# Half of the mLSTM values projected between the convolved queries and the convolved keys, with the keys' taps and SiLU moved to the end of the stage

## The chip, the cores and the metric

The kernel runs on one core of a Trainium2 chip, in one launch. The metric is the device time of that core in microseconds (us). Before the change three runs gave 661.01, 662.44 and 662.84 us, median 662.44. The engines are named as in the profile: PE (TensorE, matmuls), PEld (its weight loads), DVE (VectorE), ACT (ScalarE), POOL (GpSimd) and SP (which issues DMAs). L215 is line 215 of the kernel before. In the changed kernel most lines that are spoken of here have a number lower by one (up to L804) or higher by one (L805 to L893).

## The reference, cut to what matters

One layer over 512 tokens of width 1024. Two groups of heads read one projection of the normalised input: an mLSTM group (4 heads, whose queries and keys go through a causal convolution of four taps and a SiLU before use, while the values don't) and an attention group (8 heads, each query block attends to its best keys by an index score). A gated MLP follows, with a convolution of its own.

```
z = h @ w_in[l]
(m_q, m_k, m_v, m_o, m_i, m_f, a_q, a_k, a_v, i_q, i_k, i_w) = split_cols(z, IN_SIZES)
qk = jax.nn.silu(causal_dwconv(jnp.concatenate([m_q, m_k], axis=-1), mlstm_conv_w[l], mlstm_conv_b[l]))
...
hm = mlstm_chunkwise(m_q..., m_k..., m_v..., m_i + i_bias[l], m_f + f_bias[l])
hm = rms_norm(hm, mlstm_norm[l]) ; hm = jax.nn.sigmoid(m_o) * hm
ha = dsa_attention(a_q, a_k, a_v, i_q, i_k, i_w, rel_bias)
x = x + jnp.concatenate([hm, ha], axis=-1) @ w_out[l]
h = rms_norm(x, norm_ffn[l])
u = causal_dwconv(h @ w_up[l], ffn_conv_w[l], ffn_conv_b[l])
x = x + (jax.nn.silu(gate) * val) @ w_down[l]
```

## The kernel before

**Products in three passes.** A float32 weight is split into a high part `whi` (a copy on ACT, L124) and a low part `wlo` (a subtraction, L125, on DVE, or on POOL for the pieces 6 to 24 and a few later ones). Activations are split in the same way (`hh`, `hl`), and each product is hi*hi + lo*hi + hi*lo. Each weight tile of 256 columns gives two pieces. `fm_steps` projects 128 columns for all 512 tokens, features on partitions, in four steps of six matmuls with 512 columns (L215 to L217). `tm_steps` projects 256 columns, tokens on partitions, in eight steps of twelve matmuls with 256 columns (L259 to L261), and needs two pieces at once. Weights are loaded and split in the order in which `add_raw` lists them, ahead of use.

**The order of the work.** `merge` takes a list of main steps (a projection) and lists of side steps. Each side list has a stretch of the main list in fractions, and its steps are laid out evenly in it. A queue `later` gives up one small piece of work per step: the next weight splits and the taps of a convolution. What is written out is the order of each engine, which runs its own list strictly in that order, and waits by semaphores for the others.

**The stage that is changed.** Main steps are four convolution blocks (`to_conv`, 0 and 1 are the mLSTM queries `mq`, 2 and 3 the keys `mk`) of four steps, and then half of the values (`to_mv(0)`, eight steps). A block's last step evacuates PSUM on ACT (L785) and puts three taps on DVE in the queue (L788), each over the whole block. `silus` (both SiLUs, on ACT, and a small memset) stands at 0.7 of the stage. A SiLU and an exponential need different tables on ACT, so that each change of function is an `ACT_TABLE_LOAD`. Side work: the last steps of the top-k of query block 3 (`top3`), the gates (`gate_4` to `gate_7`), the first two `decays`, and all of the attention, `att_steps`.

**The attention** has a software pipeline: step i issues the logits of item i (a query block t and a head h; L701, L702), the biased logits `l` and their row bound `nm` of item i-1 on DVE (L726) with the exponential on ACT (L729), the transposes of item i-3 (L712, copied to `pT` on ACT at L717 or on DVE at L715), and the product with the values of item i-5 (L744). Block 3 takes its bias through `score`, which POOL adds up for each head (L737). At a block's last head DVE takes the reciprocal of the row sums (L748) and writes the output (L751), which frees the only PSUM bank of the products, `bank_av`; the next block's first product waits for it. `second` (L690) subtracts the low part of the queries on DVE.

**PSUM** has two banks `mm`, three `lg`, two `tp` and one `av`; a bank is taken in rotation of its tag. `gate_6` takes two `tp` tiles:

```
pb, pi = bank("tp"), bank("tp")
... nc.tensor.transpose(pi[:4, ...], ig[:, t, :], ident)           # L616
... nc.tensor.matmul(pb[:4, ...], lf[:, t, :], tri_u, ...)          # L618
nc.vector.tensor_tensor_scan(m, m2, pi[:4, :], 0.0, OP.add, OP.max)  # L620
nc.vector.tensor_tensor(m2, pb[:4, :], m, OP.subtract)               # L622
```

**The stage behind it** projects the other half of the values and the output gate. In it come the decays 2 and 3 (a PE broadcast L818, DVE L825 and L829, the exponential L832), the split of `mk` and `mq` into parts (`keys` L859 on ACT, `queries` L868, with subtractions on DVE), and the products `qk` (L881, L882), whose PSUM tile is taken from the three `lg` banks and read by DVE (L884, L887).

Of the kernel before, what the change touches and what calls it, by code (L numbers as in the profile page):

```python
# [28 lines left out]
def merge(main, *sides, later=None):  # L29


    order = [((i + 0.5) / len(main), 0, i, f) for i, f in enumerate(main)]
    for n, (a, b, steps) in enumerate(sides):
        cost = [getattr(f, "cost", 1.0) for f in steps]
        at = np.cumsum(cost) - 0.5 * np.array(cost)
        order += [(a + (b - a) * at[i] / sum(cost), n + 1, i, f) for i, f in enumerate(steps)]
    for _, _, _, f in sorted(order, key=lambda z: z[:3]):
        g = later.popleft() if later else None
        f()
        if g:  # L40
            g()
# [3 lines left out]
def hybrid_layer(ctx: ExitStack, tc: tile.TileContext, a, out):  # L45
# [19 lines left out]
    def mm_bank():  # L65
        mm_tags.append(mm_tags.pop(0))
        return bank(mm_tags[-1])
# [4 lines left out]
    def add_raw(pieces, cuts, place=None):  # L72

        raws.append([pieces, place])
        for view, shape in cuts:
            subs.append([len(raws) - 1, view, shape, None])
# [15 lines left out]
    def merged(main, *sides):  # L92
        merge(main, *sides, later=later)
        while later:
            later.popleft()()
# [31 lines left out]
    def cols(w, ncol, c0, width=256):  # L127
        def pieces(raw):
            dst = raw[:, :8 * width].rearrange("p (k c) -> p k c", k=8)
            src = bass.AP(tensor=w.tensor, offset=w.offset + c0, ap=[[ncol, 128], [128 * ncol, 8], [1, width]])  # L130
            return [(dst, src)]
        return pieces

    def fm_cut(j, width=256):
        return (lambda raw: raw[:, :8 * width].rearrange("p (k c) -> p k c", k=8)[:, :, j * 128:(j + 1) * 128], (8, 128))

    def tm_cut(j):
        return (lambda raw: raw.rearrange("p (k c) -> p k c", k=8)[:, 4 * j:4 * j + 4, :], (4, 256))
# [8 lines left out]
    w_in, DIN, NF = a["w_in"], 3664, DFF // 128  # L147
# [17 lines left out]
    for c0 in (1544, 1800, 2056, 2312):  # L165
        add_raw(cols(w_in, DIN, c0), [fm_cut(0), fm_cut(1)])
    add_raw(cols(w_in, DIN, 2824), [tm_cut(0), tm_cut(1)])
    for c0 in (0, 256):
        add_raw(cols(w_in, DIN, c0), [fm_cut(0), fm_cut(1)])
    for c0 in (512, 768, 1024, 1280):  # L170
        add_raw(cols(w_in, DIN, c0), [tm_cut(0), tm_cut(1)])
    for k0 in (4, 6, 0, 2):
        add_raw(rows(a["w_out"], k0), [row_cut(0), row_cut(1)])
    for c2 in range(NF // 2):
# [31 lines left out]
    def take(n=1):  # L206

        i = sub_i[0]
        sub_i[0] += n
        split_to(i + n)  # L210
        split_soon(i + n + min(look[0], 4 - n))
        return [subs[j][3] for j in range(i, i + n)]

    def mm3(ps_, lh, ll, rh, rl, first, last):
        nc.tensor.matmul(ps_, lh, rh, start=first, stop=False)  # L215
        nc.tensor.matmul(ps_, lh, rl, start=False, stop=False)  # L216
        nc.tensor.matmul(ps_, ll, rh, start=False, stop=last)  # L217

    def fm_steps(act, evac, cols_=128, tok=((0, 512),)):

        st = {}

        def open_():
            (st["w"],) = take()
            st["ps"] = mm_bank()[:cols_, :]

        def part(t0, t1, k0, k1):
            wh, wl = st["w"]
            for k in range(k0, k1):
                mm3(st["ps"][:, t0:t1], wh[:, k, :], wl[:, k, :], act[0][:, k, t0:t1], act[1][:, k, t0:t1],  # L230
                    k == 0, k == 7)

        steps = []
        for t0, t1 in tok:
            n = 2 if t1 - t0 > 256 else 4
            for k in range(0, 8, n):
                steps.append(lambda t0=t0, t1=t1, k=k, n=n: part(t0, t1, k, k + n))
        f0 = steps[0]
        steps[0] = lambda: (open_(), f0())
        last = steps[-1]  # L240
        steps[-1] = lambda: (last(), evac(st["ps"]))
        return steps

    def tm_steps(act, evac):

        st = {}
        steps = []

        def part(t, j):
            if t == 0 and j == 0:  # L250
                st["w"] = take(2)
            if j == 0:
                st["ps"] = mm_bank()[:, :256]
            sl = slice(t * 128, (t + 1) * 128)
            wh, wl = st["w"][j]
            for i in range(4):
                k = 4 * j + i
                ah, al = act[0][:, k, sl], act[1][:, k, sl]
                nc.tensor.matmul(st["ps"], ah, wh[:, i, :], start=(k == 0), stop=False)  # L259
                nc.tensor.matmul(st["ps"], al, wh[:, i, :], start=False, stop=False)  # L260
                nc.tensor.matmul(st["ps"], ah, wl[:, i, :], start=False, stop=(k == 7))  # L261
            if j == 1:
                evac(t, st["ps"])

        for t in range(NB):
            for j in range(2):
                steps.append(lambda t=t, j=j: part(t, j))
        return steps
# [100 lines left out]
    H = (hh, hl)  # L369
# [165 lines left out]
    def top_steps(t):  # L535
        w = (t + 1) * 128
        acc = score[t][:, :w]

        m8 = {}

        def largest():
            m8[0] = small.tile([128, 8], F32, name="m8")
            nc.vector.max(m8[0], acc)

        def strike():
            nc.vector.match_replace(acc, m8[0], acc, TAKEN)

        def fin():
            nc.vector.tensor_scalar(keep[t][:, :w], acc, TAKEN, -BIG, op0=OP.not_equal, op1=OP.mult)
        return [largest, strike] * 16 + [fin]  # L550
# [82 lines left out]
    gates_b = [gate_4, gate_5, gate_6, gate_7]  # L633


    main = []
# [130 lines left out]
    main = []  # L767
# [5 lines left out]
    att_ = att_steps(range(NB))  # L773
    top3 = top_steps(3)
# [7 lines left out]
    def to_conv(c):  # L782
        def evac(pz):
            y = (mq if c < 2 else mk)[:, c % 2, :]
            nc.scalar.activation(y, pz, AF.Identity, bias=cw[:, 4, c:c + 1], scale=cw[:, 3, c:c + 1])  # L785

            def tap(d):
                nc.vector.scalar_tensor_tensor(y[:, d:], pz[:, :S - d], cw[:, 3 - d, c:c + 1], y[:, d:],  # L788
                                               op0=OP.mult, op1=OP.add)
            later.extend(lambda d=d: tap(d) for d in (3, 2, 1))  # L790
        return evac

    def to_mv(c2):
        return lambda t, pz: nc.scalar.activation(mv[:, t, 2 * c2:2 * c2 + 2, :128],
                                                  pz.rearrange("p (h d) -> p h d", h=2), AF.Copy)
# [3 lines left out]
    def to_mo(c2):  # L799
        return lambda t, pz: nc.vector.tensor_copy(past[0][:, t, c2 * 256:(c2 + 1) * 256], pz)  # L800

    def silus():
        nc.gpsimd.memset(mv[:, :, :, 128:130], 1.0)
        nc.scalar.activation(mq, mq, AF.Silu)  # L804
        nc.scalar.activation(mk, mk, AF.Silu)  # L805


# [84 lines left out]
    decays, parts, qks = weight_steps()  # L892
    mm_tags[:] = ["mm"]  # L893
    main = []
    for c in range(4):
        main += fm_steps(H, to_conv(c))
    main += tm_steps(H, to_mv(0))
    merged(main, (0.0, 0.57, top3[6:]), (0.403, 0.74, gates_b), (0.781, 0.957, decays[:2]), (0.7, 0.7, [silus]), (0.007, 1.0, att_[1:]))


    def head_steps(pair):
# [47 lines left out]
    main = tm_steps(H, to_mv(1))  # L949
# [12 lines left out]
    def out_steps(mix, done, first, last, ahead=4):  # L962


        st = {}
        order = [(t, hf, j) for t in range(NB) for hf in range(2) for j in range(4)]
        if first:
            order[:8] = [(0, hf, j) for j in range(4) for hf in range(2)]
        if last:
            order[24:] = [(NB - 1, hf, j) for j in range(4) for hf in range(2)]  # L970

        def part(t, hf, j):
            if t == 0 and hf == 0 and j == 0:
                st["w"] = take(4)
            if j == 0:
                st[hf] = mm_bank()
            sl = slice(t * 128, (t + 1) * 128)
            wh, wl = st["w"][j]
            nc.tensor.matmul(st[hf], mix[:, 0, j, sl], wh[:, hf, :], start=(j == 0), stop=False)  # L979
            nc.tensor.matmul(st[hf], mix[:, 1, j, sl], wh[:, hf, :], start=False, stop=False)  # L980
            nc.tensor.matmul(st[hf], mix[:, 0, j, sl], wl[:, hf, :], start=False, stop=(j == 3))  # L981
            if t == NB - 1 and hf == 1 and j < ahead:
                split_to(nsplit[0] + 1)
            if j == 3:
                xs = x[t][:, hf * 512:(hf + 1) * 512]
                nc.vector.tensor_tensor(xs, st[hf], xs, OP.add)
                done(t, hf)
        return [lambda z=z: part(*z) for z in order]
# [3 lines left out]
    main = out_steps(mixa, lambda t, hf: None, True, True)  # L992
# [110 lines left out]
    main = g1[:2] + g0[2:] + v0[2:] + g1[2:] + fm_steps(F, to_val(1))  # L1103
# [148 lines left out]
```

## Time and profile before

| | before |
|---|---|
| median of three runs | 662.44 us (661.01 to 662.84) |
| the profiled execution | 661.26 us, of which the span from first to last instruction is 659.5 |
| mean granted clock of PE | 0.994 |
| PE busy | 640.4 us, 97% of the span, 3386 matmuls |
| DVE, ACT, POOL busy | 481.3, 317.0, 169.2 us |
| chain that ended last | PE 82%, DVE 9%, ACT 3%, POOL 2% |

The profiled execution is one run of the program with a hardware profiler. "Busy" adds up instructions; the chain is followed back from the last instruction to what released each step. The stage that is changed ends at 204.5 us of the span; its ninth main step, the first that differs, starts at 146.5 us.

### The profile page before, as it was taken

Reading aid. Unit: us, or ns where it says so; the run is one execution under the profiler, and the core shown is the slowest. Engines: PE = TensorE matmul, PEld = TensorE weight load, DVE = VectorE, ACT = ScalarE, POOL = GpSimd, SP = SyncE. Lnnn points to the kernel's source line nnn. Section 1 sums busy time; section 2 is a strip of 40 time slices with the busy share of each in tenths; the row PEclk is TensorE's granted clock in tenths of the full one; section 3 lists DMA queues with packets and bytes.
Section 4 is the critical chain, followed back from the end, with each engine's and each line's share of the span. In section 5 each row is a group of like instructions: output and inputs, shape, how many; then the busy total and the mean of one; then the engine's idle time right before and its main releaser. Section 6 shows DMA issues by size and latency. Waiting matters only on the chain.

```text
span 659.5 us, 9106 instructions
## 1 busy us (share of the span) xinstructions
PE 640.4 (97%) x3386; PEld 546.8 (83%) x3386; DVE 481.3 (73%) x864; ACT 317.0 (48%) x533; POOL 169.2 (26%) x178
## 2 busy tenths in 40 slices
PE   7999999989999999999999999999999999999994
PEld 5977889868889998889988888888888888888884
DVE  5588999979846866667457665667766678998883
ACT  5546355756675614525344244434344336665561
POOL 2232467221462405325021112121112211000011
PEclk9999999989999999999999999999999999999998
DMA  9421443120110311042354657447664665655542
GB/s 301 117 80 64 141 148 106 54 66 1 64 65 1 130 65 64 6 155 66 125 201 160 215 192 254 178 146 252 192 220 168 229 232 179 231 191 195 186 171 90
DMA packets 58027, 93.95 MB, mean 142 GB/s; under 512 B 4643, under 2 KB 41703, under 8 KB 57856
## 3 DMA queue, kind: packets, MB, share of 16 engines
q1 hardware_dynamic: 50464, 65.49, 29.9%
q0 software_dynamic: 6800, 26.32, 11.3%
q10 hardware_dynamic: 720, 1.57, 0.7%
q8 instruction: 27, 0.44, 0.3%
q14 instruction: 16, 0.13, 0.1%
HBM read 79.72 MB, written 13.65 MB: 142 GB/s over the span
## 4 chain that ended last, share of the span: by engine, by line
PE 82%; DVE 9%; ACT 3%; issue 2%; POOL 2%; DMA 1%; POOLq 0%; DVEq 0%; ACTq 0%
PE bank_mm L215 10%; PE bank_mm L216 10%; PE bank_mm L217 10%; PE bank_av L216 5%; PE bank_av L217 5%; PE bank_av L215 5%; DVE score L528 2%; PE bank_mm L396 2%; PE bank_mm L259 2%; PE bank_mm L979 2%; PE bank_mm L981 2%; PE bank_mm L980 2%; PE bank_tp L1138 2%; PE bank_mm L1138 2%; PE bank_mm L1136 2%
## 5 line engine op out<-in xcount | busy, mean ns | idle before, releaser
L124 ACT ACTIVATE whi<-raw 128x1024 fp32r<-128x1024 f32 x120 | 123.2, 1028 | 69.3 <-PE bank_av L1137 12.6
L125 DVE TENSOR_TENSOR wlo<-raw,whi 128x1024 fp32r<-128x1024 f32 x98 | 117.9, 1206 | 51.1 <-ACT whi L124 51.1
L215 PE MATMUL bank_mm<-fh,whi 128*128 128x512 f32 (+1 forms) x248 | 93.2, 376 | 0.0
L217 PE MATMUL bank_mm<-fh,wlo 128*128 128x512 f32 (+1 forms) x248 | 93.1, 376 | 0.0
L216 PE MATMUL bank_mm<-fl,whi 128*128 128x512 f32 (+1 forms) x248 | 93.1, 375 | 0.0
L125 POOL TENSOR_TENSOR wlo<-raw,whi 128x1024 fp32r<-128x1024 f32 x22 | 54.2, 2468 | 72.0 <-ACT whi L124 56.7
L1051 POOL TENSOR_TENSOR y<-yc 128x512 f32<-128x512 f32 x22 | 30.7, 1397 | 142.0 <-DVE yc L1035 142.0
L215 PEld LDWEIGHTS bank_mm<-fh,whi 128*128 128x128 f32 x248 | 46.7, 188 | 8.5
L217 PEld LDWEIGHTS bank_mm<-fh,wlo 128*128 128x128 f32 x248 | 46.7, 188 | 8.4
L216 PEld LDWEIGHTS bank_mm<-fl,whi 128*128 128x128 f32 x248 | 46.7, 188 | 8.4
L215 PE MATMUL bank_av<-fh,whi 128*128 128x512 f32 (+1 forms) x128 | 48.2, 376 | 0.0
L217 PE MATMUL bank_av<-fh,wlo 128*128 128x512 f32 (+1 forms) x128 | 48.1, 376 | 0.0
L216 PE MATMUL bank_av<-fl,whi 128*128 128x512 f32 (+1 forms) x128 | 48.1, 376 | 0.0
L215 PE MATMUL bank_mm<-hh,whi 128*128 128x512 f32 (+1 forms) x112 | 44.0, 393 | 0.0
L216 PE MATMUL bank_mm<-hl,whi 128*128 128x512 f32 (+1 forms) x112 | 42.3, 378 | 0.0
L217 PE MATMUL bank_mm<-hh,wlo 128*128 128x512 f32 (+1 forms) x112 | 42.3, 378 | 0.0
L1044 ACT ACTIVATE yc<-yc 128x512 f32<-128x512 f32 x22 | 13.9, 633 | 57.7 <-DVE yc L1035 57.7
L1094 DVE TENSOR_TENSOR prep<-prep 128x512 f32<-128x512 f32 x44 | 30.1, 685 | 3.6 <-DMA prep<-in_w_down_dram 3.3
L259 PE MATMUL bank_mm<-whi,hh 128*128 128x256 f32 x112 | 32.6, 291 | 0.0
L260 PE MATMUL bank_mm<-whi,hl 128*128 128x256 f32 x112 | 31.6, 282 | 0.0
L261 PE MATMUL bank_mm<-wlo,hh 128*128 128x256 f32 x112 | 31.6, 282 | 0.0
L1033 ACT ACTIVATE yc<-bank_mm,fw 128x512 f32<-128x512 f32 x29 | 22.3, 769 | 16.7 <-PE bank_mm L217 16.7
(363 smaller groups left out, 1572.5 us busy)
## 6 DMA issues: line engine op xcount, KB each, us to landing
raw<-in_w_up_dram SPq DMA_DIRECT2D x22, 1024.0 KB, 6.0
raw<-in_w_in_dram SPq DMA_DIRECT2D x13, 1024.0 KB, 5.0
prep<-in_w_down_dram POOLq DMA_DIRECT2D x11, 1024.0 KB, 5.4
tq<-prep POOLq DMA_DIRECT2D x11, 1024.0 KB, 4.6
raw<-tq SPq DMA_DIRECT2D x20, 512.0 KB, 4.6
raw<-in_w_down_dram SPq DMA_DIRECT2D x15, 512.0 KB, 4.3
raw<-in_w_out_dram SPq DMA_DIRECT2D x4, 1024.0 KB
T<-skew POOLq DMA_DIRECT2D x1, 2048.0 KB, 8.5
```

The lines of the kernel that those rows point to most:

```text
L124: nc.scalar.activation(hv, src, AF.Copy)
L125: (eng or nc.vector).tensor_tensor(lv, src, hv.bitcast(F32), OP.subtract)
L215: nc.tensor.matmul(ps_, lh, rh, start=first, stop=False)
L216: nc.tensor.matmul(ps_, lh, rl, start=False, stop=False)
L217: nc.tensor.matmul(ps_, ll, rh, start=False, stop=last)
L259: nc.tensor.matmul(st["ps"], ah, wh[:, i, :], start=(k == 0), stop=False)
L260: nc.tensor.matmul(st["ps"], al, wh[:, i, :], start=False, stop=False)
L261: nc.tensor.matmul(st["ps"], ah, wl[:, i, :], start=False, stop=(k == 7))
L1033: nc.scalar.activation(y, pz, AF.Identity, bias=fw[:, 3, c:c + 1], scale=fw[:, 2, c:c + 1])
L1051: nc.gpsimd.tensor_tensor(g[:, c, :], y[:, 0, :], y[:, 1, :], OP.mult)
L1094: nc.vector.tensor_tensor(prep[:, o, :], prep[:, x_, :], prep[:, y_, :], OP.subtract)
L1138: nc.tensor.matmul(b_[:, cs], gh[:, c, sl], wl[:, cs], start=False, stop=last, skip_group_check=True)
```

## The change

The values' first half (`to_mv(0)`) moves from behind the four convolution blocks to between the queries' two and the keys' two; the list of weight loads follows. `silus` is cut into `silu_q`, with the memset, at 0.6 of the stage, and `silu_k`, called once the stage is all written out.

```diff
-    for c0 in (0, 256):
-        add_raw(cols(w_in, DIN, c0), [fm_cut(0), fm_cut(1)])
-    for c0 in (512, 768, 1024, 1280):
-        add_raw(cols(w_in, DIN, c0), [tm_cut(0), tm_cut(1)])
+
+    for c0, cut in ((0, fm_cut), (512, tm_cut), (256, fm_cut), (768, tm_cut), (1024, tm_cut), (1280, tm_cut)):
+        add_raw(cols(w_in, DIN, c0), [cut(0), cut(1)])
...
-    def silus():
+    def silu_q():
         nc.gpsimd.memset(mv[:, :, :, 128:130], 1.0)
         nc.scalar.activation(mq, mq, AF.Silu)
+
+    def silu_k():
         nc.scalar.activation(mk, mk, AF.Silu)
...
-    for c in range(4):
+    for c in range(2):
         main += fm_steps(H, to_conv(c))
     main += tm_steps(H, to_mv(0))
-    merged(main, (0.0, 0.57, top3[6:]), (0.403, 0.74, gates_b), (0.781, 0.957, decays[:2]), (0.7, 0.7, [silus]), (0.007, 1.0, att_[1:]))
+    for c in range(2, 4):
+        main += fm_steps(H, to_conv(c))
+    merged(main, (0.0, 0.57, top3[6:]), (0.403, 0.74, gates_b), (0.781, 0.957, decays[:2]), (0.6, 0.6, [silu_q]), (0.007, 1.0, att_[1:]))
+    silu_k()
```

**PE, at `gate_6`.** Before, these rows stand ahead of the keys' last convolution step, with the names as in the code above (`bank_tp` is a tile of either `tp` bank); "waits" names the engine whose semaphore a row waits for.

```order
L616 MATMUL bank_tp<-ident,ig 4x128 [waits Activation_49]
L616 MATMUL bank_tp<-ident,ig 4x128 x3
L618 MATMUL bank_tp<-tri_u,lf 4x128 [waits Activation_49]
L618 MATMUL bank_tp<-tri_u,lf 4x128 x3
L701 MATMUL bank_lg<-kS,qd 128x512 [waits DVE_49]
L702 MATMUL bank_lg<-kS,ql 128x512 [waits DVE_49]
L712 MATMUL bank_tp<-ident,l 128x128 [waits DVE_49]
```

With the change the same rows stand ahead of the last step of the values.

```order
L615 MATMUL bank_tp<-ident,ig 4x128 [waits Activation_49]
L615 MATMUL bank_tp<-ident,ig 4x128 x3
L617 MATMUL bank_tp<-tri_u,lf 4x128 [waits DVE_49]
L617 MATMUL bank_tp<-tri_u,lf 4x128 x3
L700 MATMUL bank_lg<-kS,qd 128x512
L701 MATMUL bank_lg<-kS,ql 128x512
L711 MATMUL bank_tp<-ident,l 128x128 [waits Activation_49]
```

The rows themselves are in the same order; what moved is a wait. `pb` (L618 before, L617 now) waited for a copy on ACT, with `pi` in one `tp` bank and `pb` in the other. Now both tiles fall to the same bank of the two, and the row's wait points to DVE's scan, which reads `pi`.

**ACT, from the last gate on.** Before, behind `em` of `gate_7` (L630): both SiLUs with their table loads, and only then the next split of a weight (`whi`).

```order
L630 ACTIVATE em<-bank_tp 128x16 [waits PE_49]
L804 ACT_TABLE_LOAD
L804 ACTIVATE mq<-mq 128x1024
L805 ACTIVATE mk<-mk 128x1024 [waits DVE_49,Activation_49]
L124 ACTIVATE whi<-raw 128x1024 [waits DMAHW6_49]
L729 ACT_TABLE_LOAD
L729 ACTIVATE l,rs<-l,nm 128x512 [waits DVE_49]
L124 ACTIVATE whi<-raw 128x1024
```

With the change, at the same place:

```order
L629 ACTIVATE em<-bank_tp 128x16 [waits PE_49]
L124 ACTIVATE whi<-raw 128x1024 [waits DMAHW6_49]
L728 ACTIVATE l,rs<-l,nm 128x512 [waits DVE_49,Activation_49]
L716 ACTIVATE pT<-bank_tp 128x512 [waits PE_49,Activation_49]
L728 ACTIVATE l,rs<-l,nm 128x512 [waits DVE_49] x2
```

The SiLU of `mq` stands earlier (behind the exponential of block 2's head 7), that of `mk` later, and the split follows `em` at once. On POOL the `wlo` of this split stands, in both orders, behind the `score` of block 3's head 3.

**ACT, at the end of the stage.** Before, the last exponentials of the decays (`past` and `qv` are the tiles that hold decays 2 and 3) and the splits for the next stage:

```order
L832 ACTIVATE sc<-sc 128x1280 [waits DVE_49]
L794 ACTIVATE mv<-bank_mm 128x2x128 [waits PE_49]
L832 ACTIVATE past<-past 128x1280 [waits DVE_49]
L832 ACTIVATE qv<-qv 128x1280 [waits DVE_49,PE_49]
L124 ACTIVATE whi<-raw 128x1024 [waits DMAHW7_49,Pool_49]
```

With the change:

```order
L833 ACTIVATE sc<-sc 128x1280 [waits DVE_49]
L784 ACTIVATE mk<-bank_mm,cw 128x512 [waits PE_49]
L806 ACT_TABLE_LOAD [waits DVE_49]
L806 ACTIVATE mk<-mk 128x1024 [waits Activation_49]
L833 ACT_TABLE_LOAD
L833 ACTIVATE past<-past 128x1280 [waits DVE_49]
L833 ACTIVATE qv<-qv 128x1280 [waits DVE_49,PE_49]
L124 ACTIVATE whi<-raw 128x1024 [waits DMAHW7_49,Pool_49]
```

Ahead of the exponentials there now stand the evacuation of the keys' last block, a table load that waits for the block's last tap on DVE, the SiLU of `mk`, and a second table load. On DVE the three taps of this block stand between the output of the attention's last block (L751) and the decays 2 and 3.

## Rows read from the trace of the kernel before

**Rows 1.** Busy time by stretch: PE, PEld, DVE, ACT, POOL; granted clock; DMA.

```profile
146.00:206.00 60.00, 58.93 (x418) 51.59 (x417) 44.92 (x111) 36.10 (x76) 21.71 (x19) 1.00 0.11 36
206.00:247.00 41.00, 41.00 (x331) 40.23 (x331) 29.69 (x65) 19.56 (x28) 10.72 (x8) 1.00 0.22 78
```

**Rows 2.** PE's waits in the whole span: total, times, longest.

```profile
PE bank_av L744 <- DVE qv L751: 2.6, 2, 2.3
```

**Rows 3.** PE's waits from 146 to 212 us.

```profile
PE bank_lg L701 <- DVE nm L726: 0.5, 1, 0.5
PE bank_av L744 <- DVE qv L751: 0.4, 1, 0.4
```

**Rows 4.** Busy time by stretch, around the longest wait.

```profile
134.00:142.00 8.00, 5.14 (x28) 4.09 (x27) 7.36 (x22) 3.68 (x12) 3.15 (x3) 0.88 0.41 133
142.00:150.00 8.00, 8.00 (x47) 6.82 (x47) 4.97 (x13) 4.50 (x13) 0.80 (x2) 0.91 0.01 2
```

**Rows 5.** Timeline of PE: start, length, what; a step of either kind and what follows.

```profile
173.51 0.47 PE L215 MATMUL bank_mm<-hh,whi 128*128 128x512 f32 x1
...
174.97 0.39 PE L701 MATMUL bank_lg<-kS,qd 128*128 128x512 f32 x1
...
180.63 0.36 PE L259 MATMUL bank_mm<-whi,hh 128*128 128x256 f32 x1
...
182.15 0.39 PE L701 MATMUL bank_lg<-kS,qd 128*128 128x512 f32 x1
```

**Rows 6.** Timeline of all engines, 179 to 188 us, around the SiLUs.

```profile
179.35 1.28 ACT L804 ACT_TABLE_LOAD   x1
...
183.68 2.40 POOL L125 TENSOR_TENSOR wlo<-raw,whi 128x1024 fp32r<-128x1024 f32 x1 [4.91 <-ACT whi L124]
...
187.23 0.69 DVE L726 CUSTOM_DVE_ANT_0 l<-bank_lg,score 128x512 f32<-128x512 f32 x1 [4.18 <-POOL score L737]
...
187.99 0.51 PE L701 MATMUL bank_lg<-kS,qd 128*128 128x512 f32 x1 [0.54 <-DVE nm L726]
```

**Rows 7.** Timeline of all engines at `gate_6`.

```profile
171.05 1.04 PE L618 MATMUL bank_tp<-tri_u,lf 128*4 128x128 f32 x8
...
171.22 1.21 DVE L620 TENSOR_TENSOR_SCAN rows<-rows,bank_tp 4x512 f32<-4x512 f32 x1
```

**Rows 8.** Timeline of all engines where block 3 follows block 2.

```profile
179.15 0.18 ACT L630 ACTIVATE em<-bank_tp 128x16 f32<-128x16 f32 x1 [0.78 <-PE bank_tp L629]
...
181.46 0.58 DVE L690 TENSOR_TENSOR ql<-qv,qd 64x128 fp32r<-64x128 f32 x2
...
182.36 0.69 DVE L751 TENSOR_TENSOR qv<-bank_av,rr 128x512 f32<-128x512 f32 x1
...
183.11 1.10 PE L744 MATMUL bank_av<-qv,pT 128*128 128x64 f32 x8
```

**Rows 9.** Timeline of all engines, 151 to 155 us: two subtractions beside a split.

```profile
151.92 2.68 DVE L690 TENSOR_TENSOR ql<-qv,qd 64x128 fp32r<-64x128 f32 x2
152.04 2.41 POOL L125 TENSOR_TENSOR wlo<-raw,whi 128x1024 fp32r<-128x1024 f32 x1 [6.44 <-issue]
```

**Rows 10.** Timeline of DVE: a block's three taps.

```profile
177.37 2.31 DVE L788 SCALAR_TENSOR_TENSOR mk<-bank_mm,cw,mk 128x509 f32<-128x509 f32 x3
```

**Rows 11.** Timeline of ACT, 180 to 224 us: a SiLU; the end of the stage.

```profile
181.61 1.04 ACT L805 ACTIVATE mk<-mk 128x1024 f32<-128x1024 f32 x1
...
207.31 1.27 ACT L832 ACTIVATE past<-past 128x1280 f32<-128x1280 f32 x1 [3.20 <-DVE past L829]
...
210.57 1.04 ACT L124 ACTIVATE whi<-raw 128x1024 fp32r<-128x1024 f32 x1
...
223.37 0.60 ACT L124 ACTIVATE mixa<-bank_tp 128x512 fp32r<-128x512 f32 x1
```

**Rows 12.** Timeline of all engines, 226 to 229 us: two of the `qk` products.

```profile
226.72 0.55 DVE L887 SCALAR_TENSOR_TENSOR sc<-bank_lg,sc 128x384 f32<-128x384 f32 x1
...
228.50 0.28 PE L881 MATMUL bank_lg<-part 128*128 128x256 f32 x1
```

## The prediction

> **What bounds the kernel now.** I looked first at busy time by stretch. From 146.5 us on, where the first main step differs, PE is busy 58.93 of the 60 us to 206 and all of the 41 us behind it [rows 1]. So this stage is bound by PE, as the whole kernel is, and idle time of DVE, ACT and POOL costs nothing until PE waits for it. The list of PE's waits comes next: of all its waits for the bank of the products only the longest, 2.3 us, is large, and it lies at 138 us [rows 2], ahead of everything the change moves. From 146 to 212 us two waits are left, 0.5 and 0.4 us [rows 3]. The reader is to see the size of the prize: the change can't win more than these, and the 1.07 us that PE idles there in all. Everything else that it can do is to make a wait.
>
> A wait may cost more than its length. In the 8 us around the longest one PE's granted clock was 0.88, and 0.91 in the next 8 [rows 4], where 1.00 stands for the higher of its levels, 2.4 GHz: 0.12 and 0.09 of 8 us are 1.7 us lost besides the wait. From 146 to 247 us it is 1.00 [rows 1].
>
> **The change, part by part. The steps themselves** cost nothing more or less: six matmuls of 512 columns and what stands behind them start 1.46 us apart (173.51 to 174.97), twelve of 256 columns 1.52 us apart (180.63 to 182.15) [rows 5]. Blocks of PE work trade places, and the side steps keep theirs, since they are placed by fractions. What can change is who is late. I went through the waits of PE in the new order one by one and set the times of before against them.
>
> *First, the wait at 187.99 us goes: -0.7.* PE waits 0.54 us for the row bound of block 3's head 4 [rows 6], since DVE waited 4.18 us for POOL's `score`, which stood behind a `wlo` that began at 183.68, which waited for a `whi` behind both SiLUs, whose first table load starts at 179.35 [rows 6]. With the change `whi` follows `em` at once, and this `wlo` begins some 3 us earlier. The wait is 0.54 us, and the idle of the whole stretch 1.07, of which the other wait keeps 0.4: 0.7 is what belongs to this place with the small gaps beside it. Ends: -0.5 and -1.07.
>
> *Second, `gate_6`: +1.4.* Before, `pb` begins at 171.05, while the scan that reads `pi` runs on DVE from 171.22 for 1.21 us [rows 7]. Now `pb` has the bank of `pi` and waits for the scan: 171.22 + 1.21 = 172.43, later by 1.38, and with the way from DVE to PE 1.4. PE runs its list in order, so it all falls on PE. The SiLU of the queries, which now stands on ACT just here, is hidden behind this: its copy of `pT` comes at about 173.3 and is asked for at about 174. Ends: 1.2 (DVE has no taps left here and begins the scan a little sooner, but not before `pi` is written) and 1.8.
>
> *Third, the passage from block 2 to block 3: +1.4.* Before, DVE's `ql` at 181.46 takes 0.58 us for two, the output is written from 182.36 to 183.05, and PE's first product of block 3 comes at 183.11: there is no slack [rows 8]. Now `whi` follows `em`, which ended at 179.33 [rows 8], and with 1.04 us for it [rows 11] `wlo` starts on POOL at about 180.4 and runs 2.4 us, to 182.85. The trace shows what that does to `ql`: at 151.92 the same two subtractions took 2.68 us, and ended at 154.60, just behind a `wlo` that ran on POOL from 152.04 to 154.45 [rows 9]. So `ql` would end near 183.4 and not 182.04: 1.4 later, and so does PE. What decides is whether `wlo` starts before `ql` does; by the sum it leads by 1.0 us. Ends: 0 and 2.1.
>
> The Trainium skill has a rule for this ("SBUF — State Buffer", section "Who interferes with whom"): a DVE instruction with two SBUF inputs contends with a GpSimd instruction that reads SBUF, the one that starts first holds the shared port for the whole instruction, and the other is blocked. The trace agrees for `ql` beside `wlo`, 2.68 for 0.58 us.
>
> *Fourth, two splits on end: +0.2.* The values need two pieces at once, so that two `wlo` follow each other on POOL at about 152 to 157 us, where one stood. DVE's small sums of `gate_4` and the next `ql` wait for the second, and block 1's output comes later, for which PE already waits 0.4 us [rows 3]. A `wlo` of 2.4 us that holds `ql` cost it up to 2.1 there [rows 9], but only its tail reaches this place, and DVE does three taps less in this part, 2.31 us [rows 10]. Ends: 0 and 0.8; I take 0.2, near the lower.
>
> *Fifth, the end of the stage: +1.7.* Before, ACT's exponential of decay 2 starts at 207.31, that of decay 3 follows, and the split of the next weight starts at 210.57 [rows 11]. Now the last block's three taps, 2.31 us [rows 10], stand ahead of the decays on DVE, and on ACT a table load (1.28 [rows 6]), the SiLU (1.04 [rows 11]) and another load, the first after the last tap. Counted from PE's end of the stage, the attention's last output ends on DVE at 205.2, the taps at 207.5; the load to 208.8, the SiLU to 209.9, the load to 211.2; two exponentials of 1.27 to 213.5. The split moves from 210.57 to 213.53, by 2.96 us. From there to 223.97 ACT ran row behind row (splits, the parts of `mk` and `mq`, copies out of PSUM; 19 rows, of which the first, at 210.57, and the last, at 223.37 for 0.60, stand in [rows 11]), so that the delay arrives whole at the products `qk`. The fourth, at 228.50, takes the `lg` bank of the first, which DVE gives back at 226.72 + 0.55 = 227.27 [rows 12]: a slack of 1.23. So PE waits 2.96 - 1.23 = 1.7. Ends: 0.8 (the DVE chain alone, 2.31 of taps, would leave 1.1, and ACT may close up a little) and 2.3 (the exponentials too wait a little longer).
>
> The Trainium skill prices a change of tables higher ("ScalarE: Activation LUTs", section "What ACT_TABLE_LOAD costs"): about 1283 ns for the load and about 1380 ns to drain, some 2.66 us. By that page the two loads would add an estimated 2.8 us to this chain, and PE would wait some 4.5 us. The trace has 1.28 us for each, with the next instruction right behind.
>
> **The sum**: -0.7 + 1.4 + 1.4 + 0.2 + 1.7 = +4.0 us on the profiled execution's 661.26 (a span of 659.5 and 1.8 around it): 665.3. That run is 1.2 below the median of the three, so that a median of 662.44 becomes **666.4**. All lower ends together give -1.07 + 1.2 + 0.8 = +0.9, all upper ones -0.5 + 1.8 + 2.1 + 0.8 + 2.3 = +6.5.
>
> **The rivals.**
>
> *A, no difference that can be told (+0 to +2).* About 0.3%, 2.0 us, is what a measurement of this kernel can tell from no change. If the third part doesn't come (DVE reaches `ql` before `wlo` starts; a lead of 1.0 us is all that speaks against it), 2.6 are left; if the fifth comes out at 0.8 because ACT's pieces close up, 3.1; with both, 1.7, at 664.1. With the lower ends of the others it falls to 663.3. For it: each of these is a chain of five or more steps, on two engines that I moved by sums; against it: `gate_6` is certain by the order, and the seam by DVE's taps alone.
>
> *B, faster (661.4).* DVE, busy 44.92 of the 60 us from 146 to 206 [rows 1], loses the taps of the keys in the middle of it; the waits at 159 and 188 us go, and all of the 1.07 us of idle is won; and `gate_6`'s `pb` costs nothing. That would need the scan to be done when `pb` comes, before 171.05; by [rows 7] it can't begin before `pi` is written, at about that time. If it decided, and neither seam waited, the time would be 662.44 - 1.07 = 661.4, which is not yet faster by 0.3%. To come to 660.4 the 1.7 us of clock around 138 us would have to be won as well, and the orders are the same there.
>
> *C, slower by more (668.1).* One of the new waits of 1.4 to 1.7 us drops the clock, as the 2.3 us did. One such dip adds its 1.7 [rows 4] to the sum: 668.1, two 669.8. Against it: the waits of 0.4 to 0.5 us left the clock at 1.00 [rows 1], and the new ones lie 12 and 45 us apart.
>
> *D, dearer table loads.* If each of the two loads at the end of the stage holds ACT for twice its row, 1.28 us more [rows 6], PE waits 2.6 us longer: 669.0. Against it: one load, two SiLUs and a `whi` are 1.28 + 3 x 1.04 = 4.4 us by their rows, and the `wlo` behind them begins 4.33 us after the load does [rows 6, 11], which leaves no room for more. The Trainium skill's page on ScalarE, as above, speaks for it.
>
> **How the numbers follow.** The forecast, two or three of the waits with a sum of 2 to 5 us, has 0.57; A 0.26; B 0.05; C 0.09, D 0.03. The predicted time is that of the forecast. The range leaves out B, the lower half of A, and the ends of C and D: from 663.0 to 668.7. Slower by over 0.3% is above 664.4: most of the forecast and of C and D, 0.67; within 0.3%, A and the low end of the forecast, 0.28; faster, below 660.4, 0.05.
>
> **What would show it.** In the profile of the changed kernel: no wait of PE for `nm` at 188 us (first); `pb` waiting 1.4 us at about 171 for the scan (second); a `ql` of about 2 us beside a `wlo` just ahead of the last block's first product, and PE waiting for L750 there (third); ACT with a load, a SiLU and a load at what was 207 to 211 us before, its split of the next weight 3 us later, and PE waiting for DVE's L888 at the fourth `qk` (fifth). The prediction is wrong if PE's waits from 146 to 247 us sum to less than 2 or more than 7 us, if the granted clock falls below 0.97 there, or if the time outside this stretch changes.

## The result: 0.7% slower, by the waits that were forecast and one loss of clock

| | before | changed |
|---|---|---|
| median, five runs each | 661.01 us | 666.81 us |
| lowest and highest | 659.18, 662.84 | 665.41, 667.13 |
| ratio, 95% interval | | 1.0072 (1.0058 to 1.0086) |
| profiled execution: span, mean clock | 659.5 us, 0.994 | 665.3 us, 0.990 |

666.81 lies in the range of 663.0 to 668.7 and beside the 666.4 that was forecast. Two more runs of the kernel before moved its median from 662.44 to 661.01, so that the change costs 4.8 us by the ratio, 5.8 between the medians and between the two profiles; 4.0 were forecast.

Where the time went is seen in PE's waits of the changed kernel, 146 to 250 us (line, releaser: total, times, longest), which answer to [rows 3]:

```profile
PE bank_av L743 <- DVE qv L750: 2.4, 2, 2.0
PE bank_lg L882 <- DVE sc L888: 1.4, 1, 1.4
PE bank_tp L617 <- DVE rows L619: 1.4, 1, 1.4
```

The wait for `nm` at 188 us is gone, and three others have come: at `gate_6`, at the passage from block 2 to block 3, and at the fourth `qk`. Busy time by stretch, with the columns of [rows 1]:

```profile
134.00:142.00 8.00, 5.14 (x25) 4.05 (x24) 7.06 (x22) 3.38 (x11) 3.15 (x3) 0.84 0.41 133
146.00:206.00 60.00, 56.28 (x394) 49.16 (x393) 41.87 (x101) 34.50 (x72) 21.61 (x19) 0.97 0.06 18
182.00:190.00 8.00, 6.03 (x28) 4.96 (x28) 4.98 (x9) 2.23 (x5) 4.50 (x3) 0.82 0.00 0
190.00:198.00 8.00, 8.00 (x52) 6.73 (x51) 3.87 (x12) 2.78 (x6) 2.33 (x2) 0.96 0.00 0
206.00:252.00 46.00, 44.52 (x349) 42.84 (x348) 33.18 (x70) 23.61 (x31) 10.98 (x9) 1.00 0.26 92
```

PE idles 60 - 56.28 = 3.72 and 46 - 44.52 = 1.48 us, 5.2 together, where it idled 1.07 before [rows 1]: 4.1 more. The rest is clock: 0.82 and 0.96, from 182 to 198 us, are 0.18 x 8 + 0.04 x 8 = 1.8 us. 4.1 + 1.8 = 5.9, against 5.8 between the spans.

The rows of the three waits, from the timeline of all engines:

```profile
171.21 1.21 DVE L619 TENSOR_TENSOR_SCAN rows<-rows,bank_tp 4x512 f32<-4x512 f32 x1 [3.18 <-PE bank_tp L615]
172.47 0.71 PE L617 MATMUL bank_tp<-tri_u,lf 128*4 128x128 f32 x5 [1.37 <-DVE rows L619]
...
181.78 2.40 POOL L125 TENSOR_TENSOR wlo<-raw,whi 128x1024 fp32r<-128x1024 f32 x1 [2.06 <-ACT whi L124]
182.89 2.61 DVE L689 TENSOR_TENSOR ql<-qv,qd 64x128 fp32r<-64x128 f32 x2
184.14 1.21 POOL L736 TENSOR_TENSOR score<-T,keep 128x512 f32<-128x512 f32 x1
185.82 0.69 DVE L750 TENSOR_TENSOR qv<-bank_av,rr 128x512 f32<-128x512 f32 x1
186.56 1.44 PE L743 MATMUL bank_av<-qv,pT 128*128 128x64 f32 x8 [1.97 <-DVE qv L750]
...
211.12 1.28 ACT L806 ACT_TABLE_LOAD   x1 [3.05 <-DVE mk L787]
212.41 1.06 ACT L806 ACTIVATE mk<-mk 128x1024 f32<-128x1024 f32 x1
213.49 1.28 ACT L833 ACT_TABLE_LOAD   x1
...
214.79 1.27 ACT L833 ACTIVATE past<-past 128x1280 f32<-128x1280 f32 x1
...
217.13 1.04 ACT L124 ACTIVATE whi<-raw 128x1024 fp32r<-128x1024 f32 x1
...
233.97 0.36 PE L882 MATMUL bank_lg<-part 128*128 128x256 f32 x1 [1.38 <-DVE sc L888]
```

The second group holds more than was foreseen. The row of `ql` is two subtractions, which a narrower view of DVE's timeline shows one by one:

```profile
182.89 1.44 DVE L689 TENSOR_TENSOR ql<-qv,qd 64x128 fp32r<-64x128 f32 x1
184.34 1.16 DVE L689 TENSOR_TENSOR ql<-qv,qd 64x128 fp32r<-64x128 f32 x1
```

The first is held by `wlo`, and ends just behind it (184.18); the second is held by the `score` of head 4, which POOL begins at 184.14 and ends at 185.35. Together they take 2.61 us, for 0.58 in [rows 8]: about 1.1 more by `wlo` and 0.9 by `score`. Before, that `score` stood on POOL behind a `wlo` that itself waited for the SiLUs [rows 6], and could not come near `ql`.

### The profile page after: what moved, and what is told of

Read it like the earlier page. It is cut to its first block, busy times and chain, and to the rows that moved or that the text cites. A ratio compares the mean times of both kernels' runs of the same rounds, so it can differ in the third digit from the quotient of the medians.

```text
span 665.3 us, 9109 instructions
## 1 busy us (share of the span) xinstructions
PE 642.0 (96%) x3386; PEld 547.7 (82%) x3386; DVE 482.1 (72%) x864; ACT 319.7 (48%) x535; POOL 169.3 (25%) x178
## 4 chain that ended last, share of the span: by engine, by line
PE 82%; DVE 10%; ACT 4%; issue 1%; POOL 1%; DMA 1%; POOLq 0%; DVEq 0%; ACTq 0%
PE bank_mm L214 11%; PE bank_mm L216 11%; PE bank_mm L215 11%; PE bank_av L215 5%; PE bank_av L216 5%; PE bank_av L214 5%; PE bank_av L743 2%; DVE score L527 2%; PE bank_mm L395 2%; DVE ql L689 2%; PE bank_mm L984 2%; PE bank_mm L983 2%; PE bank_mm L985 2%; PE bank_tp L1142 2%; PE bank_tp L1141 2%; PE bank_mm L1142 2%
## 5 line engine op out<-in xcount | busy, mean ns | idle before, releaser
L124 ACT ACTIVATE gh<-y 128x256 fp32r<-128x256 f32 (+2 forms) x17 | 10.3, 614 | 40.5 <-POOL y L1055 40.5
```

The lines of the kernel that those rows point to most:

```text
L124: nc.scalar.activation(hv, src, AF.Copy)
```

## The experiments

All ratios are to the kernel before. The theory is that of the forecast, separate waits of PE, each with its own cause. The main rival is that the two further table loads on ACT are the cost, wherever they stand.

**The queries' SiLU earlier.**

```diff
-    merged(main, ..., (0.6, 0.6, [silu_q]), ...)
+    merged(main, ..., (0.45, 0.45, [silu_q]), ...)
```

> The changed kernel with the queries' SiLU at 0.45 of the stage instead of 0.6, so that it no longer stands on ACT ahead of gate_6. Theory (separate waits of PE, each with its own cause): pb again lies in the other tp bank than pi and waits for a copy on ACT alone, so the wait of 1.37 us at gate_6 goes; the wait of 2.0 us for the output of block 2 beside a wlo on POOL stays, with its dip of the clock, and so does the end of the stage. 1.4 us less than the changed kernel, some 3.4 above the kernel before. Rival (what costs is the two further table loads on ACT, wherever they stand): no less than the changed kernel, some 4.8 above the kernel before.

Measured: 666.65 us, ratio 1.0088 (1.0073 to 1.0103). The wait at `gate_6` is gone: `pb` runs from 173.11 beside the scan of `pi`, which begins at 173.29, so the two lie in two banks. But the time didn't fall. Its SiLU makes a wait of its own, as the timeline of all engines shows:

```profile
160.34 1.28 ACT L728 ACT_TABLE_LOAD   x1
...
161.64 0.61 ACT L728 ACTIVATE l<-l,nm 128x384 f32<-128x384 f32 x1
...
162.40 0.55 PE L711 MATMUL bank_tp<-ident,l 128*128 128x128 f32 x3 [0.60 <-ACT l L728]
```

An exponential stands behind the second load, and a transpose waits for it. With that, 0.7 us of idle are saved between the two profiles, less than the 1.7 us that the clock cost more around 138 us in this one (0.71 and 0.86 over 8 us each; last section). A miss: the bank was right, and that the place at 0.45 is free was wrong. The time alone would fit the rival of the table loads; PE's waits, and the run with the SiLUs split below, do not.

**The split ahead of `em`**, so that `wlo` starts sooner.

```diff
     def gate_7():
-        pm2 = bank("tp")
+        split_to(nsplit[0] + 1); pm2 = bank("tp")
```

> The changed kernel with the split of the next weight written ahead of em in gate_7 instead of behind it, so that whi need not wait for PE's gate and wlo runs on POOL some 2 us sooner. Theory (DVE's ql is held by a wlo on POOL that began before it): wlo ends before ql begins, ql takes 0.6 us instead of 2.6, the wait of 2.0 us goes, and with it the clock of 0.82 in the 8 us around it (1.5 to 1.8 us); the wait at gate_6 stays at 1.4. 3 to 3.8 us less than the profile of the changed kernel, some 1.3 to 2.3 above the kernel before. Rival (the output of block 2 is late since ACT's exponentials and copies are late behind the table loads): the wait stays at 2 us, and the time stays that of the changed kernel.

Measured: 664.38 us, ratio 1.0050 (1.0037 to 1.0064). That is some 3.3 us above the kernel before, where 1.3 to 2.3 were expected: the wait fell from 1.97 to 0.85, not to 0. From 146 to 250 us the clock stayed at 1.00. Timeline of all engines:

```profile
180.21 2.38 POOL L125 TENSOR_TENSOR wlo<-raw,whi 128x1024 fp32r<-128x1024 f32 x1 [0.69 <-ACT whi L124]
...
182.70 1.49 DVE L689 TENSOR_TENSOR ql<-qv,qd 64x128 fp32r<-64x128 f32 x2
182.86 1.17 POOL L736 TENSOR_TENSOR score<-T,keep 128x512 f32<-128x512 f32 x1 [0.28 <-DVE nm L725]
```

With `wlo` out of the way `ql` meets `score` alone, and loses 0.9 us to it, as in the changed kernel. The wait is one of two holds, 1.1 by `wlo` and 0.9 by `score`; the forecast knew the first. The second could have been read ahead of it from the timeline of the kernel before, where a `ql` lost 0.9 us beside a `score`:

```profile
175.24 1.49 DVE L690 TENSOR_TENSOR ql<-qv,qd 64x128 fp32r<-64x128 f32 x2
175.40 1.17 POOL L737 TENSOR_TENSOR score<-T,keep 128x512 f32<-128x512 f32 x1 [3.00 <-DVE nm L726]
```

**Both edits.**

> The two edits together: queries' SiLU at 0.45, and the split ahead of em. Theory: the savings add up; what is left is the wait at 188 us that the change took away (-0.7) and the end of the stage (+1.4 to 1.9), so 0.7 to 1.2 above the kernel before, and a granted clock of 1.00 from 146 us on. Rival of the table loads: some 4.8 above the kernel before.

Measured: 664.10 us, ratio 1.0044 (1.0029 to 1.0058), some 2.9 us above the kernel before for an expected 0.7 to 1.2. The difference is that of the two waits just found, here 0.7 at 161 us and 1.0 at the passage.

**The SiLUs split in the order of before.**

```diff
         nc.scalar.activation(mq, mq, AF.Silu)
-        nc.scalar.activation(mk, mk, AF.Silu)
+    def silu_k(): nc.scalar.activation(mk, mk, AF.Silu)
...
-    merged(main, ..., (0.7, 0.7, [silus]), ...)
-
+    merged(main, ..., (0.6, 0.6, [silus]), ...)
+    silu_k()
```

> The kernel before, in its order of projections, with the two SiLUs split as in the change: the queries' at 0.6, the keys' behind the stage. It has the change's two further table loads but neither its order nor the keys' taps at the end. Theory: gate_6 has the wait of 1.4 us (its pb falls into the bank of pi here too, because of the SiLU ahead of it on ACT), the wait of 0.5 to 0.7 at 188 us goes, the wait beside wlo does not come since the split doesn't follow em here, and the end of the stage costs PE nothing, because ACT sits idle there for 3.2 us and the two loads and the SiLU take 3.6: 0.7 to 1.0 above the kernel before. Rival of the table loads: most of the change's loss comes with them, 3.5 or more above the kernel before.

Measured: 662.25 us, ratio 1.0020 (1.0010 to 1.0030). It has both table loads more than before, and loses 0.2%, some 1.3 us, so the loads are not the cost as such. PE's waits from 146 to 250 us:

```profile
PE bank_tp L618 <- DVE rows L620: 1.4, 1, 1.4
PE bank_av L744 <- DVE qv L751: 1.2, 2, 0.8
```

`gate_6` waits here too, without any change to the projections: the SiLU ahead of it on ACT is what puts `pb` into the bank of `pi`. So the `tp` banks are not dealt out in plain rotation, as the description of the kernel has it, since two tiles taken one after the other would then never share one; how a bank is chosen no run shows. The end of the stage costs nothing. The 0.8 us at the passage were not expected; it is `score` beside `ql` again (`ql` takes 1.49 us), now without a `wlo`.

**`ql` behind a block's output, in the changed kernel.** In a step of the attention the call of `second` goes from ahead of the products to the step's end, behind L747 and L750.

```diff
-            if i and i % 2 == 0 and i // 2 + 1 < n // 2:
-                second(i // 2 + 1)
...
                     nc.vector.tensor_tensor(ha[t]..., po..., rr..., OP.mult)
+            if i and i % 2 == 0 and i // 2 + 1 < n // 2:
+                second(i // 2 + 1)
```

> The changed kernel with DVE's ql written behind the output of a query block instead of ahead of it, nothing else. Theory (the output of block 2 is late by 2.0 us because ql, which reads two operands from SBUF, is held on DVE first by wlo and then by score on POOL, and the output stands behind it; the output itself reads PSUM and is not held): PE's wait at the passage to block 3 goes though wlo runs where it did, the wait of 0.4 us at 159 goes, and the one of 2.25 us at 138, which the kernel before has too, falls by the 1.4 us that ql takes there to some 0.8. 3.8 us less than the changed kernel in waits alone, and 1.5 to 3 more where the clock no longer drops. Rival (the output is late because exponentials or copies on ACT are): no change. Rival (ql is then late itself and PE waits for it at the next logits): the wait comes back at the logits, L701 of the kernel before.

Measured: 659.49 us, ratio 0.9974 (0.9965 to 0.9983): 1.0% below the changed kernel, and faster than the kernel before. Timeline of all engines:

```profile
178.44 2.40 POOL L125 TENSOR_TENSOR wlo<-raw,whi 128x1024 fp32r<-128x1024 f32 x1 [2.08 <-ACT whi L124]
...
179.85 0.69 DVE L748 TENSOR_TENSOR qv<-bank_av,rr 128x512 f32<-128x512 f32 x1
...
180.46 1.70 DVE L689 TENSOR_TENSOR ql<-qv,qd 64x128 fp32r<-64x128 f32 x2
180.80 1.21 POOL L734 TENSOR_TENSOR score<-T,keep 128x512 f32<-128x512 f32 x1
181.09 1.00 PE L741 MATMUL bank_av<-qv,pT 128*128 128x64 f32 x8
```

`wlo` and `score` run where they did and hold `ql` for 1.1 us; the output, which reads PSUM and a small tile, takes 0.69 beside `wlo` and is there in time. PE waits for neither the output nor `ql`; the 1.4 us at `gate_6` and at the fourth `qk` are all that is left of its waits from 146 to 250 us. Only DVE's order was edited, so that late exponentials or copies on ACT are ruled out as the cause.

**The same in the kernel before.**

> The same edit in the kernel before. Its wait at 138 us falls from 2.26 to about 0.8, the one of 0.36 at 159 goes, the passage to block 3 had none. 1.8 us less than the kernel before in waits, and up to 1.7 more if the clock stays up around 138 us: 0.9945 to 0.9975 of the kernel before.

Measured: 658.70 us, ratio 0.9963 (0.9949 to 0.9977), as expected. The wait at 138 us fell from 2.26 to 0.81. `pb` now waits 0.6 us for `pT` on ACT, and the wait at 188 us grew from 0.5 to 0.7.

**The end of the stage, in two halves**: the changed kernel without the keys' SiLU, and the changed kernel without the last block's taps. The first:

```diff
-    silu_k()
```

The second:

```diff
-            later.extend(lambda d=d: tap(d) for d in (3, 2, 1))
+            later.extend(lambda d=d: tap(d) for d in ((3, 2, 1) if c < 3 else ()))
```

> The changed kernel without the SiLU of the keys (the keys are left without their SiLU; its two table loads go with it). Theory for the end of the stage (taps on DVE ahead of the decays, and ACT's load, SiLU and load, overlap only in part): the exponentials then start when the decays are done, some 1.7 us sooner, the split of the next weight 0.8 us sooner, and PE's wait at the fourth qk falls from 1.4 to about 0.6; about 0.8 to 1 us less than the changed kernel. Rival (the loads and the SiLU on ACT are the whole cost): the wait goes to 0, 1.9 us less.

> The changed kernel without the three taps of the keys' last block (the convolution of that block keeps only its first term), with its SiLU. Theory: the table load follows the evacuation of PSUM at once, the second load ends before DVE's decays do or with them, the split of the next weight comes 3 us sooner, as before the change, and PE's waits at the end of the stage go: 1.4 to 1.9 us less than the changed kernel. Rival (ACT's loads and SiLU are the whole cost): the wait stays.

Measured: 666.33 us, 1.0082 (1.0067 to 1.0096), and 664.47 us, 1.0053 (1.0036 to 1.0071). Without the SiLU PE's wait at the fourth `qk` falls from 1.38 to 0.97, without the taps to none. The first ACT rows of each (without the SiLU; then without the taps):

```profile
212.98 1.27 ACT L833 ACTIVATE past<-past 128x1280 f32<-128x1280 f32 x1 [5.03 <-DVE past L830]
...
216.25 1.04 ACT L124 ACTIVATE whi<-raw 128x1024 fp32r<-128x1024 f32 x1
```

```profile
209.62 1.28 ACT L806 ACT_TABLE_LOAD   x1
210.91 1.06 ACT L806 ACTIVATE mk<-mk 128x1024 f32<-128x1024 f32 x1
211.99 1.28 ACT L833 ACT_TABLE_LOAD   x1
```

Without the SiLU the exponentials wait for DVE's decays, which stand behind the taps. Without the taps the loads run while DVE writes the decays, and hide. So the taps make the delay, and the loads with the SiLU add 0.4 us to it. That is less than the 0.8 expected; the timed ratio of the first (1.0082 beside 1.0072) does not show it, its interval being wider than the saving. The second is 1.3 us below the changed kernel by the ratios, for an expected 1.4 to 1.9.

**The queries' SiLU later**, at 0.64, behind `gate_6` and ahead of `em`; alone, and with `ql` last.

> The changed kernel with the queries' SiLU at 0.64 of the stage instead of 0.6: behind gate_6 on ACT, ahead of em. Theory: pb lies in the other tp bank than pi again, so no wait at gate_6 (-1.4); em comes some 2 us later on ACT, behind the SiLU's two loads, and with it the split, so that wlo begins on POOL behind the start of ql, and the score of head 4, which would hold ql too, stands behind wlo in POOL's order: ql is held by neither, and the wait of 2.0 us at the passage to block 3 goes with its dip of the clock. What is left against the kernel before is the end of the stage (+1.4 to 1.9) and the wait at 188 us that is gone (-0.7): 1.0010 to 1.0025 of the kernel before. If ql were held whenever wlo runs at some time near it, the wait would stay at 0.8 to 2 us.

> The changed kernel with the queries' SiLU at 0.64 and with ql behind a block's output. Of the waits from 146 to 250 us only the one at the end of the stage is left (1.4), the one at 138 is 0.8, and the clock stays at 1.00: 1.4 us less than the changed kernel with ql last alone, 0.994 to 0.996 of the kernel before.

Measured: 663.16 us, ratio 1.0018 (1.0010 to 1.0027), and 659.98 us, 0.9965 (0.9953 to 0.9978). Alone, with the timeline of all engines:

```profile
182.84 0.58 DVE L689 TENSOR_TENSOR ql<-qv,qd 64x128 fp32r<-64x128 f32 x2
...
183.95 2.37 POOL L125 TENSOR_TENSOR wlo<-raw,whi 128x1024 fp32r<-128x1024 f32 x1 [3.90 <-ACT whi L124]
...
184.49 1.10 PE L743 MATMUL bank_av<-qv,pT 128*128 128x64 f32 x8
...
186.28 1.17 POOL L736 TENSOR_TENSOR score<-T,keep 128x512 f32<-128x512 f32 x1
```

A later SiLU makes `wlo` late, `score` stands behind it, and `ql` meets neither: 0.58 us. Moving one instruction from 0.6 to 0.64 takes back 0.5%, two of the three waits. What is left of the loss is the end of the stage, 1.4 us.

With `ql` last the later SiLU was expected at 0.994 to 0.996, 1.4 us less than `ql` last alone; it is 0.6 us less by the ratios and 0.5 more by the medians, so that no saving is shown. PE's waits went as expected, with only the 1.4 us at the end of the stage left. But in this profile the clock was 0.79 from 134 to 142 us, where it was 1.00 with `ql` last alone, which takes back 1.7 us; three of the seven runs lie at 658.4 to 658.6 us, the other four at 660.0 to 660.1.

**Everything in the order of before**: `ql` last, the queries' SiLU at 0.64, the keys' behind the stage.

> The kernel before with its order of projections, ql behind a block's output, the queries' SiLU at 0.64 and the keys' behind the stage (so the keys' taps come in the middle, as before the change). Theory: the wait of 0.7 at 188 us goes as with the change, pb and pi lie in two banks (0 to 0.6 for a copy on ACT), the end of the stage costs nothing since the taps aren't there; 0.5 to 1.3 us less than the kernel before with ql last alone, 0.993 to 0.9965 of the kernel before.

Measured: 658.04 us, ratio 0.9948 (0.9936 to 0.9960), the lowest of all, though its interval overlaps with that of the kernel before with `ql` last alone. The wait at 188 us is gone, as with the change; three small ones, 0.3 to 0.6 us, remain from 146 us on.

## Why the prediction was right

- **First term, -0.7.** Right: no wait for `nm` near 188 us.
- **Second, +1.4.** Right to the row: 1.37. That the bank comes from where the queries' SiLU stands on ACT was not in the prediction; two experiments show it (in the order of before with the SiLU at 0.6 `pb` waits, in the changed order with it at 0.64 it doesn't).
- **Third, +1.4.** The mechanism was right, the size short: 1.97. `wlo` led `ql` by 1.1 us (1.0 forecast) and cost it about 1.1, but `score` held `ql` as well, for 0.9. The measured value lies inside the ends that were kept, 0 and 2.1.
- **Fourth, +0.2.** It came out at 0: the wait at 159 us is 0.38, for 0.36 before. The lower end was the answer.
- **Fifth, +1.7.** The wait is 1.38, and 0.1 lies ahead of it. Nearly right, and by the chain that was named: the last tap, then load, SiLU, load. (The prediction's own terms, two exponentials of 1.27 from 211.2, end at 213.7 and not at 213.5, which would have made its wait 1.9.)
- **The sum** of the waits, +4.0, was measured as 4.1, since the third term's miss upwards and those of the fourth and fifth downwards nearly cancel. No sign of being wrong came: the clock from 146 to 247 us was 0.98, and the waits lie between 2 and 7 us. What makes the profile's 5.8 is rival C, to which a chance of 0.09 was given: behind the wait of 2 us at the passage the clock fell, for 1.8 us. In this stage only the wait of 2.0 us did that, in all four profiles that have it: behind those of 1.37 and 1.38 in the same profile, and behind the 0.85 with the split ahead of `em`, the clock stayed at 1.00. So it probably came because the third term was longer than forecast; but length alone doesn't decide, as the 0.8 us at 138 us show (last section).
- **That the time came so close is luck.** The 666.4 starts from a median of 662.44, which is 1.4 us above that of the five runs, and its sum lacks the 1.8 us of clock; the two errors nearly cancel.
- **Rival D** fell: each load took 1.28 us, and the next instruction began 0.01 and 0.02 us behind it. The Trainium skill's drain ("ScalarE: Activation LUTs", section "What ACT_TABLE_LOAD costs"), which by the prediction's estimate would have made some 4.5 us of the wait at the end, does not show in this trace.

## What to carry to other kernels

When a long two-operand instruction on POOL can start just ahead of a two-operand instruction on DVE, look at what stands behind the latter on DVE; what frees a bank for PE goes first. An instruction that is late may be shielding another from such a hold: here the SiLUs held up `wlo` and `score`, and moving them away exposed `ql`. And a move on one engine can change which bank a tile of PE gets: look at each wait's releaser in the new order, not only at the order of the rows.

## What the runs showed of the hardware

The wait at 138 us, up to which the orders are the same in all kernels but those with `ql` last, costs a different time in different executions. In the profiles of the changed kernel and of the one with the SiLU at 0.64 PE waits 2.25 us there; in the first the clock is 0.84 from 134 to 142 us and 0.95 in the next 8 us, 1.7 us lost, in the second:

```profile
134.00:142.00 8.00, 5.13 (x21) 3.98 (x20) 7.26 (x21) 3.60 (x12) 3.15 (x3) 0.71 0.41 133
142.00:150.00 8.00, 8.00 (x53) 7.22 (x52) 3.93 (x11) 3.82 (x12) 0.80 (x2) 0.86 0.01 2
```

0.29 and 0.14 of 8 us are 3.4 us lost. With `ql` last the wait is 0.8 us, and the clock stayed at 1.00 there in the profile of the changed order, but was 0.79 in that of the order of before. What decides it no run shows. The runs of the kernel before fall apart in the same way, most of them at 660.6 to 661.2 us with a mean clock of 0.993 or 0.994, or at 661.7 to 662.7 with 0.991 or 0.992. So a difference of 1.5 us between two single runs of these kernels is not yet the work of an edit.
